# A plain first block by token halves in the inner SwiGLUs, TensorE's order at the norms written out, and turned tiles split straight from PSUM

## The chip, the cores and the metric

The kernel runs on one core of a Trainium2 chip. Its time is the device time of one execution in microseconds, and a version is judged by the median of its runs. The profiled execution is one further run, with its own time and span.

The engines in the profile are PE (TensorE, matrix products and transposes; PEld is its loading of weights), DVE (VectorE), ACT (ScalarE), POOL (GpSimd) and SP (SyncE). SP issues most loads; POOL issues loads and the DMAs that add into a tile.

## The reference

The input x is 512 tokens of 1024 features, in fp32. There are two layers, and a final norm.

```python
def rms_norm(x, gain):
    inv = lax.rsqrt(jnp.mean(xf * xf, axis=-1, keepdims=True) + NORM_EPS)
    return (xf * inv).astype(x.dtype) * gain

def swiglu(h, w_gate, w_up, w_down):
    return (jax.nn.silu(h @ w_gate) * (h @ w_up)) @ w_down

for l in range(DEPTH):
    x = x + 0.5 * swiglu(rms_norm(x, ffn1_norm[l]), ffn1_wg[l], ffn1_wu[l], ffn1_wd[l])
    h = rms_norm(x, mix_norm[l])
    z = h @ w_in[l]
    ...
    x = x + jnp.concatenate([attn_out, conv_out], axis=-1) @ w_out[l]
    x = x + 0.5 * swiglu(rms_norm(x, ffn2_norm[l]), ffn2_wg[l], ffn2_wu[l], ffn2_wd[l])
return rms_norm(x, final_norm)
```

The hidden width of a SwiGLU is 2816. The mixing between the two SwiGLUs of a layer is a sliding-window attention beside a short convolution.

## The kernel before

**Numbers.** Every fp32 operand of a matrix product is kept as two parts, hi (a rounded copy, written by ACT) and lo (the rest, a subtraction on DVE); `split` (L203 to L205) makes them. A product is three matmuls: hi by hi, hi by lo, lo by hi. Weights come by DMA into tiles `raw` (8 buffers, `need_raw`, L190) and are split into `wh` and `wl` (3 buffers each, `need_split`, L213, with the split at L204 and L205). A unit of weights is 512 KB. `split_far` (L207 to L211) makes lo in another way: ACT writes hi and the negated source, and a DMA issued by POOL adds the source to it.

**Stages.** The 2816 hidden columns are 11 blocks of 256. A SwiGLU is a list of stages (L32 to L40). `p` is a plain block (gate and up, four groups of 128 columns over all eight chunks of 128 features). `w` is a pair of blocks done with seven half-size products instead of eight (`winograd2`, L926), in the order of CHAINS: the accumulators x, w, x, y, x, y, x take the operands b11, b21, t2, t3, t1, t4, b22. The operands are quarters of the normed, turned activations (chunks 0 to 3 or 4 to 7, first or second half of the 512 tokens), and t1 to t4 are sums of quarters; `Seven.make` (L567) forms and splits one, once. `u` is one block done in the same way with matmuls of 256 columns (`winograd`, L867, matmuls at L896). `s` is the down-projection of four blocks, again with seven products (`share`, L790, through `stream`, L775, matmuls at L781). `d` is the plain down-projection of the blocks listed (`down`, L300, matmuls at L309). Three SwiGLUs use INNER (FFN2 of layer 0, FFN1 and FFN2 of layer 1; the last with another ending, LAST, whose list is the same); FFN1 of layer 0 uses FIRST. Where a `w` block's result is needed with the features on the partitions, `turn` (L979) transposes it on TensorE, and `flush` empties the list of turns that wait, some per step.

**The norm.** `Norm` is called after each piece of the residual stream x is final (L504): ACT squares it with a row sum (L506). When the four pieces of one half of the tokens are there, `stage` (L522) forms the root (L529 to L532), and for each of the four pieces `turn` (L541) scales it (xn, L546, DVE), transposes it in four blocks into a PSUM tile (L551) and copies the tile out: to the full tile hf for a SwiGLU (L557, on ACT or DVE), or split into hh and hl for the mixing. For a SwiGLU, `stage` then makes b11 and b21 from the first half, and t2 after the second.

**PSUM.** The pools are "mm" (4 banks), "sc" (2) and "aux" (2). The tiles of the eight turns take their banks from a list of tags (L1385, L1386): aux, aux, sc, sc for the first half, then mm, mm, sc, sc ahead of a SwiGLU and sc, sc, aux, aux ahead of the mixing.

**The mixing** (`mix`, L1177) runs its first three groups of w_in by token halves: all three over the first 256 tokens, then all three over the second (L1186 to L1199, matmuls of 256 columns). Its output projection is a `share` whose operands t1, t4 and b22 are split far (L1181). The pieces of x that it ends go to the next norm: that is where FFN2's norm begins, during the last steps of `share`.

**Order.** The tile framework's scheduler decides in which order each engine gets its instructions, here for PE too; only the last stage of all has its order on ACT and DVE written by hand (L1160).

Of the kernel before, what the change touches and what calls it, by code (L numbers as in the profile page):

```python
# [15 lines left out]
P = 128  # L16
# [20 lines left out]
    ("w", 0), ("w", 2), ("w", 4), ("w", 6), ("w", 8), ("u", 10), ("s", 0), ("s", 4),  # L37
    ("d", (8, 9, 10)),
)
LAST = INNER[:-1] + (("d", (8, 9, 10)),)  # L40
# [32 lines left out]
def trunk_kernel(  # L73
# [226 lines left out]
    def down(acts, blocks):  # L300
# [167 lines left out]
    class Norm:  # L468
# [19 lines left out]
        def rooms(self):  # L488
            if self.mixing:
                self.parts = [  # L490
# [7 lines left out]
            else:  # L498
# [3 lines left out]
                self.make, self.forms = self.seven.make, self.seven.forms  # L502

# [18 lines left out]
        def stage(self, half):  # L522

            i = self.i
            if half == 0:
                self.rooms()
            v, r, y = (small(f"{n}_{i}_{half}", 2) for n in "vry")
# [5 lines left out]
            for o in range(2):  # L533
                for t in (at, at + 1):
                    self.turn(t, o, y[:, t - at : t - at + 1])
                if half == 0 and not self.mixing:
                    self.make(("b11", "b21")[o])
            if half and not self.mixing:
                self.make("t2")

        def turn(self, t, o, by):  # L541
# [3 lines left out]
            xn = g2(f"xn_{name}")  # L545
            nc.vector.scalar_tensor_tensor(  # L546
                xn, xt(t, o), by, self.gain[o], op0=ALU.mult, op1=ALU.mult
            )
# [3 lines left out]
            if self.mixing:  # L552
                hi, lo = (p[:, :, tok] for p in self.parts[o])
                nc.scalar.copy(hi, tp)
                nc.vector.tensor_sub(lo, tp, f32(hi))
            else:
                (nc.vector.tensor_copy if o else nc.scalar.copy)(self.full[o][:, :, tok], tp)  # L557
# [217 lines left out]
    def stream(accs, wh, wl, xh, xl, h, start):  # L775

        for u in range(2):
            tok = slice(u * P, (u + 1) * P)
            for k in range(2):
                for i, (x_, w) in enumerate(((xh, wh), (xl, wh), (xh, wl))):  # L780
# [7 lines left out]
                    )  # L788

    def share(ops, by, between=None, soon=None, after=None):  # L790
# [34 lines left out]
    def ffn(norm, stages, whole, after=None, late=None):  # L825
# [4 lines left out]
        def plain(b):  # L830
# [34 lines left out]
            acts[b] = (hi, lo)  # L865

# [59 lines left out]
        def winograd2(b, between=None):  # L926
# [12 lines left out]
            for step, (acc, operand, start) in enumerate(CHAINS):  # L939
# [32 lines left out]
                if not first and step < 4:  # L972
# [452 lines left out]
```

## Time and profile before

| what | value |
|---|---|
| median of 3 runs | 1727.09 us (1723.63 to 1728.24) |
| the profiled execution | 1727.49 us |
| its span in the profile | 1725.7 us |
| mean granted TensorE clock | 0.992 |
| instructions | 21836 |

A line of the timeline gives start, duration, engine, line of the program, operation, the tile written and the tiles read, and in brackets the idle time of the engine just before it with what ended it. Names lose their buffer numbers: `ft_m` is any of the sums t1 to t4 of the mixing's projection, `fb_m` a plain quarter of it, `y_s` an accumulator of a down-projection share, `w`, `x` and `y` those of a pair of blocks, `acc` that of a plain group. "x2" after a line counts neighbouring instructions of one form, which the view merges even where other matmuls lie between. A duration of a matmul includes its way through the array, so the time that one costs in a row is the distance between two starts. A row of the windows view gives, for a stretch, the busy time and the count of instructions of each engine, the granted clock, the DMA share and the rate.

### The profile page before, as it was taken

The page shows a single profiled execution, that of the slowest core. Times are in us where ns is not written, and L with a number is a line of the kernel's source. Part 1 is how long each engine was busy: PE and PEld are TensorE (multiplying, and loading weights), DVE is VectorE, ACT ScalarE, POOL GpSimd, SP SyncE. Part 2 cuts the span into 40 slices and gives each one's busy share as a digit, 9 for nine tenths or more (in the row PEclk, how much of TensorE's full clock was granted, in tenths as well). Part 3 has the DMA queues.
Part 4 walks back from the last instruction along what each step waited for, and adds up shares of the span by engine and source line. Part 5 has one row for each costly group of instructions (what it writes and reads, how often), then busy time and mean ns, then how long its engine had stood idle before and what let it go on. Part 6 is the DMA issues. An engine that isn't in the chain of part 4 may idle for free.

```text
span 1725.7 us, 21836 instructions
## 1 busy us (share of the span) xinstructions
PE 1685.2 (98%) x8150; PEld 1405.2 (81%) x8150; DVE 1345.7 (78%) x1762; ACT 959.5 (56%) x1369; POOL 191.8 (11%) x172
## 2 busy tenths in 40 slices
PE   9999999999988999999999999999999799999998
PEld 7888898898867888887778888878888678888877
DVE  7986689868779777799597776995578797776994
ACT  6545555556565555564455555644565655556553
POOL 0011111000210111011101111110002101111101
PEclk9999999999999999999999999999999989999999
DMA  8467788622694767678547776783127947767781
GB/s 244 103 180 194 183 205 210 166 66 62 153 225 123 207 172 189 179 191 222 147 122 196 186 180 184 191 219 112 39 74 166 212 133 191 188 171 190 189 207 49
DMA packets 188206, 285.62 MB, mean 166 GB/s; under 512 B 9124, under 2 KB 72132, under 8 KB 188100
## 3 DMA queue, kind: packets, MB, share of 16 engines
q1 hardware_dynamic: 146340, 204.91, 37.6%
q0 software_dynamic: 41056, 78.65, 26.9%
q8 instruction: 64, 1.05, 0.2%
q10 hardware_dynamic: 704, 0.66, 0.1%
q14 instruction: 42, 0.34, 0.1%
HBM read 268.46 MB, written 2.10 MB: 157 GB/s over the span
## 4 chain that ended last, share of the span: by engine, by line
PE 59%; DVE 6%; issue 2%; ACT 1%; DMA 1%; POOL 0%; ACTq 0%; POOLq 0%; DVEq 0%
PE x L781 18%; PE y L781 9%; PE x_s L781 6%; PE w L781 4%; PE y_s L781 4%; PE down L309 3%; PE x L896 2%; PE acc L291 2%; PE acc L292 2%; PE acc L294 2%; PE at L982 2%; DVE wl L205 1%; PE y L896 1%; DVE raw L231 1%; PE acc L1192 1%
## 5 line engine op out<-in xcount | busy, mean ns | idle before, releaser
L204 ACT CAST wh<-raw 128x1024 fp32r<-128x1024 f32 (+1 forms) x503 | 524.4, 1045 | 557.4 <-PE x L781 137.6
L205 DVE TENSOR_TENSOR wl<-raw,wh 128x1024 fp32r<-128x1024 f32 (+1 forms) x503 | 606.6, 1213 | 269.1 <-ACT wh L204 267.5
L781 PE MATMUL x<-wh,ft 128*128 128x512 f32 x608 | 189.6, 392 | 1.0 <-DVE ft L205 1.0
L781 PE MATMUL x<-wh,fb 128*128 128x512 f32 x608 | 188.5, 390 | 0.0
L781 PE MATMUL y<-wh,ft 128*128 128x512 f32 x608 | 188.5, 391 | 0.0
L781 PEld LDWEIGHTS x<-wh,ft 128*128 128x128 f32 x608 | 113.1, 188 | 25.1 <-DVE ft L205 2.2
L781 PEld LDWEIGHTS x<-wh,fb 128*128 128x128 f32 x608 | 114.3, 188 | 23.4
L781 PEld LDWEIGHTS y<-wh,ft 128*128 128x128 f32 x608 | 113.1, 188 | 22.7
L781 PE MATMUL x<-wl,fb 128*128 128x512 f32 x304 | 118.6, 390 | 0.0
L781 PE MATMUL x<-wl,ft 128*128 128x512 f32 x304 | 118.4, 390 | 0.0
L781 PE MATMUL y<-wl,ft 128*128 128x512 f32 x304 | 118.3, 389 | 0.0
L199 POOL DMA_DIRECT2D raw<-in_ffn_wu_dram x42 | 51.1, 1217 | 585.6 <-DMA raw<-in_ffn_wu_dram 405.2
L781 PE MATMUL w<-wh,fb 128*128 128x512 f32 x304 | 98.6, 409 | 5.3 <-ACT wh L204 5.3
L291 PE MATMUL acc<-hh,wh 128*128 128x512 f32 x240 | 94.6, 394 | 0.0
L294 PE MATMUL acc<-hh,wl 128*128 128x512 f32 x240 | 93.9, 391 | 0.0
L292 PE MATMUL acc<-hl,wh 128*128 128x512 f32 x240 | 93.6, 390 | 0.0
L309 PE MATMUL down<-wh,a 128*128 128x512 f32 x288 | 90.0, 392 | 0.0
L781 PE MATMUL y_s<-wh,ft_s 128*128 128x512 f32 x256 | 80.5, 392 | 5.4 <-ACT wh L204 5.4
L781 PE MATMUL x_s<-wh,ft_s 128*128 128x512 f32 x256 | 78.1, 393 | 1.2 <-ACT wh L204 1.0
L199 POOL DMA_DIRECT2D raw<-in_ffn_wg_dram x42 | 50.9, 1219 | 244.6 <-DVE wl L205 92.3
L781 PE MATMUL x_s<-wh,fb_s 128*128 128x512 f32 x240 | 74.0, 389 | 0.0
L781 PEld LDWEIGHTS w<-wh,fb 128*128 128x128 f32 x304 | 57.4, 195 | 19.6 <-ACT wh L204 8.2
(313 smaller groups left out, 3451.3 us busy)
## 6 DMA issues: line engine op xcount, KB each, us to landing
raw<-in_ffn_wu_dram SPq DMA_DIRECT2D x129, 512.0 KB, 3.7
raw<-in_ffn_wd_dram SPq DMA_DIRECT2D x104, 512.0 KB, 5.4
raw<-in_ffn_wg_dram SPq DMA_DIRECT2D x86, 512.0 KB, 5.0
raw<-in_ffn_wu_dram POOLq DMA_DIRECT2D x42, 512.0 KB, 7.7
raw<-in_ffn_wg_dram POOLq DMA_DIRECT2D x42, 512.0 KB, 6.3
raw<-in_w_in_dram SPq DMA_DIRECT2D x36, 512.0 KB, 3.8
raw<-in_ffn_wd_dram POOLq DMA_DIRECT2D x32, 512.0 KB, 7.8
raw<-raw POOLq DMA_DIRECT2D x20, 512.0 KB, 6.4
```

The costliest lines, as they stand in the source:

```text
L199: nc.gpsimd.dma_start(out=r, in_=rows_of(*more), accum_op=ALU.add)
L204: nc.scalar.copy(hi, raw)
L205: eng.tensor_sub(lo, raw, f32(hi))
L231: nc.vector.tensor_add(a11, a11, s1)
L291: nc.tensor.matmul(acc, hi[:, k, :], rhs[k][0], start=k == first, stop=False)
L292: nc.tensor.matmul(acc, hi[:, k, :], rhs[k][1], start=False, stop=False)
L294: nc.tensor.matmul(acc, lo[:, k, :], rhs[k][0], start=False, stop=k == last)
L309: nc.tensor.matmul(acc, a[:, k, tok], w[:, k, :], start=i + k + n == 0, stop=i == last and k == 1 and n == 2,)
L781: nc.tensor.matmul(accs[u], x_[:, 2 * h + k, tok], w[:, k, :], start=start and h + k + i == 0, stop=h + k == 2 and i == 2, skip_group_chec ...
L896: nc.tensor.matmul(out, w[:, k, cols], x_[:, k, :], start=start and k + i == 0, stop=k == KC // 2 - 1 and i == 2, skip_group_check=not start,)
L982: nc.tensor.transpose(tp[:, t * P : (t + 1) * P], ups[t][:, c * P : (c + 1) * P], ident)
L1192: nc.tensor.matmul(opened[j][:, tok], w[:, k, :], x_, start=t + k + i == 0, stop=k == KC - 1 and i == 2, skip_group_check=True,)
```

## The change

The list INNER begins with a plain block (0), five pairs follow (1, 3, 5, 7, 9), the shares cover blocks 1 to 4 and 5 to 8, and the plain down-projection takes 0, 9 and 10. The `u` stage is gone from these three SwiGLUs.

A new function `halves` runs three groups by token halves, as the mixing did, and serves both: after the second group of the first half, and in the middle of the third, it calls `norm.pull`. The plain block (`plain_halves`) is these three groups (two gates, one up), and then the second up group.

`stage` now makes the xn of a half at once and leaves the turns to `pull`, which does one pair of turns. The pulls stand in the program's order at fixed places: in the last step of the share that ends the stream (after each of its four runs of six matmuls), or after the pieces of the last down-projection, and in `halves`. From step 4 of that share, or from the second half of the down-projection, to the end of the plain block (or of the three groups of the mixing), TensorE's order is the program's (`by_hand` to `by_itself`).

A turned tile ahead of a SwiGLU is split from its PSUM bank: ACT copies hi, DVE subtracts lo, both into the operand b11, b21, b12 or b22, and ACT copies the tile in full into hf as well, for the sums. t2, t3 and t1 are made as the plain block's groups end, t4 after it. In the mixing's projection t4 is no longer split far.

In the second of the shares, the turns of the last pair (9) are flushed one per step in steps 2 to 5, into an "aux" bank.

```diff
@@ -34,10 +34,10 @@
     ("s", 2), ("d", (10,)), ("s", 6),
 )
 INNER = (
-    ("w", 0), ("w", 2), ("w", 4), ("w", 6), ("w", 8), ("u", 10), ("s", 0), ("s", 4),
-    ("d", (8, 9, 10)),
+    ("p", 0), ("w", 1), ("w", 3), ("w", 5), ("w", 7), ("w", 9), ("s", 1), ("s", 5),
+    ("d", (0, 9, 10)),
 )
-LAST = INNER[:-1] + (("d", (8, 9, 10)),)
+LAST = INNER[:-1] + (("d", (0, 9, 10)),)
 FORMS = ("a11", "a12", "s2", "s3", "s1", "a22", "s4")
 EARLY = ("a11", "a12", "s3", "s2", "a22", "s1", "s4")
 SCORES_AT = (5, 6, 7, 8, 9, 10, 12, 13)
@@ -297,7 +297,38 @@
                 nc.tensor.matmul(acc, lo[:, k, :], rhs[k][0], start=False, stop=k == last)
         return acc
 
-    def down(acts, blocks):
+    def by_hand():
+        state["region"] = tc.manual_schedule(engines={pe})
+        state["region"].__enter__()
+
+    def by_itself():
+        state["region"].__exit__(None, None, None)
+
+    def halves(norm, n, done):
+
+        first = state["group"]
+        held = [take_split(SPLIT_AHEAD - j)[1:] for j in range(n)]
+        accs = [psum("mm", [P, S], f"acc_{first + j}") for j in range(n)]
+        for t in range(2):
+            for j, (hi, lo) in enumerate(held):
+                for k in range(KC):
+                    xh, xl = norm.half(k, t)
+                    for i, (w, x_) in enumerate(((hi, xh), (hi, xl), (lo, xh))):
+                        nc.tensor.matmul(
+                            accs[j][:, t * H : (t + 1) * H],
+                            w[:, k, :],
+                            x_,
+                            start=t + k + i == 0,
+                            stop=k == KC - 1 and i == 2,
+                            skip_group_check=True,
+                        )
+                    if t == 0 and (j, k) in ((1, KC - 1), (2, KC // 2 - 1)):
+                        norm.pull()
+                if t:
+                    need_split(first + j + 3)
+                    done(j, accs[j])
+
+    def down(acts, blocks, norm=None):
 
         last = len(blocks) - 1
 
@@ -316,6 +347,8 @@
 
         for o in range(2):
             accs = [psum("mm", [P, S], f"down_{state['group']}_{t}") for t in range(NT)]
+            if o and norm:
+                by_hand()
             if o and last:
                 held = [take_split(SPLIT_AHEAD - i)[1:] for i in range(last + 1)]
                 ahead = state["group"]
@@ -328,6 +361,8 @@
                         products(accs[t], t, i, *w)
                         if i == last:
                             yield t, o, accs[t]
+                            if norm:
+                                norm.pull()
                     need_split(ahead + i)
                 continue
             for i in range(last + 1):
@@ -487,6 +522,7 @@
 
         def rooms(self):
             if self.mixing:
+                self.half = lambda k, t: [z[:, t * H : (t + 1) * H] for z in self.h[k]]
                 self.parts = [
                     [
                         xpool.tile([P, KC // 2, S], F32R, tag="xf", bufs=8, name=f"h{n}_{self.i}_{o}")
@@ -500,6 +536,9 @@
                 self.full = full
                 self.seven = Seven(full, room_g8, f"{self.i}")
                 self.make, self.forms = self.seven.make, self.seven.forms
+                self.half = lambda k, t: [
+                    z[:, k % 4, :] for z in self.forms[f"b{k // 4 + 1}{t + 1}"]
+                ]
 
         def __call__(self, t, o):
 
@@ -524,6 +563,7 @@
             i = self.i
             if half == 0:
                 self.rooms()
+                self.waiting = []
             v, r, y = (small(f"{n}_{i}_{half}", 2) for n in "vry")
             at = 2 * half
             nc.vector.tensor_add(v, self.ss[:, at : at + 2], self.ss[:, NT + at : NT + at + 2])
@@ -531,30 +571,46 @@
             nc.vector.tensor_scalar(v, v, 1.0 / D, EPS, op0=ALU.mult, op1=ALU.add)
             newton(y, r, v)
             for o in range(2):
+                xns = []
                 for t in (at, at + 1):
-                    self.turn(t, o, y[:, t - at : t - at + 1])
-                if half == 0 and not self.mixing:
-                    self.make(("b11", "b21")[o])
-            if half and not self.mixing:
-                self.make("t2")
-
-        def turn(self, t, o, by):
+                    xns.append(g2(f"xn_{i}_{t}_{o}"))
+                    nc.vector.scalar_tensor_tensor(
+                        xns[-1],
+                        xt(t, o),
+                        y[:, t - at : t - at + 1],
+                        self.gain[o],
+                        op0=ALU.mult,
+                        op1=ALU.mult,
+                    )
+                self.waiting.append((half, o, xns))
+
+        def pull(self):
+
+            if not self.waiting:
+                return
+            half, o, xns = self.waiting.pop(0)
+            for t, xn in enumerate(xns):
+                self.turn(2 * half + t, o, xn)
+
+        def turn(self, t, o, xn):
 
             name = f"{self.i}_{t}_{o}"
             tok = slice(t * P, (t + 1) * P)
-            xn = g2(f"xn_{name}")
-            nc.vector.scalar_tensor_tensor(
-                xn, xt(t, o), by, self.gain[o], op0=ALU.mult, op1=ALU.mult
-            )
             tp = psum(self.tags.pop(0), [P, KC // 2, P], f"xt_{name}")
             for j in range(KC // 2):
                 nc.tensor.transpose(tp[:, j, :], xn[:, j * P : (j + 1) * P], ident)
             if self.mixing:
                 hi, lo = (p[:, :, tok] for p in self.parts[o])
-                nc.scalar.copy(hi, tp)
-                nc.vector.tensor_sub(lo, tp, f32(hi))
             else:
-                (nc.vector.tensor_copy if o else nc.scalar.copy)(self.full[o][:, :, tok], tp)
+                what = f"b{o + 1}{t // 2 + 1}"
+                if what not in self.forms:
+                    self.forms[what] = both(f"f{what}_{self.i}")
+                at = t % 2 * P
+                hi, lo = (p[:, :, at : at + P] for p in self.forms[what])
+            nc.scalar.copy(hi, tp)
+            nc.vector.tensor_sub(lo, tp, f32(hi))
+            if not self.mixing:
+                nc.scalar.copy(self.full[o][:, :, tok], tp)
 
     class Seven:
 
@@ -772,7 +828,7 @@
                 bias[:, h, :], df, -(2.0 ** -(h + 1)), m0, op0=ALU.mult, op1=ALU.add
             )
 
-    def stream(accs, wh, wl, xh, xl, h, start):
+    def stream(accs, wh, wl, xh, xl, h, start, norm=None):
 
         for u in range(2):
             tok = slice(u * P, (u + 1) * P)
@@ -786,6 +842,8 @@
                         stop=h + k == 2 and i == 2,
                         skip_group_check=not start,
                     )
+            if norm:
+                norm.pull()
 
     def share(ops, by, between=None, soon=None, after=None):
 
@@ -794,13 +852,15 @@
         chains, shares = (CHAINS_EARLY, SHARES_EARLY) if after else (CHAINS, SHARES)
         for step, (acc, operand, start) in enumerate(chains):
             ops.make(operand)
+            if after and step == 4:
+                by_hand()
             xh, xl = ops.forms[operand]
             if start:
                 tag = {"x": "mm", "y": "sc", "w": "aux", "z": "mm"}[acc]
                 accs[acc] = [psum(tag, [P, S], f"{acc}_{ops.name}_{m}") for m in range(2)]
             for h in range(2):
                 _, wh, wl = take_split()
-                stream(accs[acc], wh, wl, xh, xl, h, start)
+                stream(accs[acc], wh, wl, xh, xl, h, start, after if step == 6 else None)
                 if soon:
                     ops.make(*soon.get((step, h), ()))
                 if h == 0:
@@ -863,6 +923,43 @@
                 norm.make("t2")
                 up(1, accs[3])
             acts[b] = (hi, lo)
+
+        def plain_halves(b):
+
+            gates = [g2(f"gate_{whole}_{b}_{j}") for j in range(2)]
+
+            def up(j, acc):
+                nc.vector.tensor_mul(gates[j], acc, gates[j])
+                if not j:
+                    acts[b] = both(f"a_{whole}_{b}", shape=(P, 2, 2, S))
+                hi, lo = acts[b]
+                split(hi[:, j, :], lo[:, j, :], gates[j])
+
+            def done(j, acc):
+                if j < 2:
+                    nc.scalar.activation(gates[j], acc, AF.Silu)
+                else:
+                    up(0, acc)
+                norm.make(("t2", "t3", "t1")[j])
+
+            halves(norm, 3, done)
+            _, hi, lo = take_split()
+            acc = psum("mm", [P, S], f"up_{whole}_{b}")
...
+            up(1, acc)
+            by_itself()
+            norm.make("t4")
 
...
@@ -969,8 +1066,6 @@
                             nc.scalar.activation(gates[2 + u], out, AF.Silu)
                             nc.vector.tensor_mul(ups[2 + u], ups[2 + u], gates[2 + u])
                 turns(step)
-                if not first and step < 4:
-                    norm.make(("t3", "t1", "t4", "b22")[step])
                 if between:
                     between(step)
             if b in blocks:
@@ -1031,9 +1126,14 @@
                     ops, 0.5, ahead(then, {3: ("b11",), 4: ("b21",), 5: sums[:1], 6: sums[1:]})
                 )
             elif what == "s":
-                share(then, 0.5, after=after if final else None)
+                share(
+                    then,
+                    0.5,
+                    None if first else lambda step: 2 <= step < 6 and flush(1, "aux"),
+                    after=after if final else None,
+                )
             if what == "p":
-                plain(b)
+                (plain if first else plain_halves)(b)
                 if b == 0 and late:
                     turn_rows(1)
             if what != "d":
@@ -1043,8 +1143,8 @@
                     [(acts[k][0][:, j, :], acts[k][1][:, j, :]) for k in b for j in range(2)]
                 )
                 return
-            for n, (t, o, acc) in enumerate(down(acts, b)):
-                if b == (0,):
+            for n, (t, o, acc) in enumerate(down(acts, b, after if final else None)):
+                if b == (0,) and first:
                     norm.make(*{0: ("t3",), 4: ("t1",)}.get(n, ()))
                 nc.vector.scalar_tensor_tensor(
                     xt(t, o), acc, 0.5, xt(t, o), op0=ALU.mult, op1=ALU.add
@@ -1178,27 +1278,12 @@
         q = [None] * NH
 
         mixed = [g8(f"m_{l}_{j}", F32, (P, KC // 2, S)) for j in range(2)]
-        ops = Seven(mixed, room_g8, f"m_{l}", far=("t1", "t4", "b22"))
-
-        first = state["group"]
-        held = [take_split(SPLIT_AHEAD - j) for j in range(3)]
-        kacc, vacc, qacc = opened = [psum("mm", [P, S], f"acc_{n}") for n, _, _ in held]
...
+        ops = Seven(mixed, room_g8, f"m_{l}", far=("t1", "b22"))
+
+        opened = []
+        halves(norm, 3, lambda j, acc: opened.append(acc))
+        by_itself()
+        kacc, vacc, qacc = opened
 
         kh, kl = both(f"k_{l}", shape=(P, 2, NKV, S))
         kh, kl = ([t[:, g, :] for g in range(NKV)] for t in (kh, kl))
```

More of the change, by code (lines that the diff above doesn't have):

```diff
@@ L865, in plain @@
             acts[b] = (hi, lo)
+        def plain_halves(b):
[15 more added lines that the diff above has]
+            acc = psum("mm", [P, S], f"up_{whole}_{b}")
+            for t in range(2):
+                for k in range(KC):
+                    xh, xl = norm.half(k, t)
+                    for i, (w, x_) in enumerate(((hi, xh), (hi, xl), (lo, xh))):
+                        nc.tensor.matmul(
+                            acc[:, t * H : (t + 1) * H],
+                            w[:, k, :],
+                            x_,
+                            start=t + k + i == 0,
+                            stop=k == KC - 1 and i == 2,
+                            skip_group_check=True,
+                        )
+            up(1, acc)
+            by_itself()
+            norm.make("t4")
         def winograd(b, between):
```

17 lines of the change are left out of this document (1 added, 16 removed).

## The prediction

> **What bounds the kernel now.** The page first:
>
> ```profile
> span 1725.7 us, 21836 instructions
> PE 1685.2 (98%) x8150; PEld 1405.2 (81%) x8150; DVE 1345.7 (78%) x1762; ACT 959.5 (56%) x1369; POOL 191.8 (11%) x172
> PE   9999999999988999999999999999999799999998
> PEclk9999999999999999999999999999999989999999
> PE 59%; DVE 6%; issue 2%; ACT 1%; DMA 1%; POOL 0%; ACTq 0%; POOLq 0%; DVEq 0%
> ```
>
> TensorE (PE) sets the time: it is busy for 98% and carries 59% of the chain that ended last. Its row has dents at slices 11 and 12 and near slice 32, and the clock row has one at the latter. So two questions decide: how much matmul time the change adds, and what happens in the dents. For the first I need pitches, start to start, from the timeline and from the list of one line (duration: min/median/max):
>
> ```profile
> 720.29 0.39 PE L781 MATMUL x<-wl,fb 128*128 128x512 f32 x1
> 720.97 0.39 PE L781 MATMUL x<-wl,fb 128*128 128x512 f32 x1
> 729.90 0.28 PE L896 MATMUL w<-fb,wl 128*128 128x256 f32 x1
> 730.26 0.28 PE L896 MATMUL w<-fb,wl 128*128 128x256 f32 x1
> 353.00 0.60 PE L551 MATMUL xt<-ident,xn 128*128 128x128 f32 x4
> L551 PE MATMUL xt<-ident,xn x160: 270/273/421, 337.7 to 1390.8; 128*128 128x128 f32 x160
> ```
>
> Between the first two rows, as between the next two, lie three starts (one hi·lo triple): 0.68/3 = 0.227 us for 512 columns, 0.36/3 = 0.120 us for 256. Four transposes last 0.60 us, one 0.27: (0.60-0.27)/3 = 0.11 us each.
>
> For the second, three stretches of the windows view (PE busy with count, then PEld, DVE, ACT, POOL, clock, DMA share, GB/s), around the norms ahead of l0's FFN2, l1's FFN1 and l1's FFN2:
>
> ```profile
> 475.00:550.00 75.00, 64.07 (x272) 50.41 (x272) 64.31 (x80) 46.52 (x66) 7.85 (x7) 0.93 0.69 164
> 850.00:900.00 50.00, 46.17 (x205) 36.12 (x205) 45.74 (x57) 30.35 (x41) 3.61 (x3) 0.97 0.33 88
> 1325.00:1400.00 75.00, 64.59 (x269) 50.85 (x269) 61.50 (x76) 42.70 (x58) 12.48 (x11) 0.91 0.72 162
> ```
>
> Each holds the norm's 32 transposes (8 turned tiles of four), the rest are 512 wide. At full pitch the first needs 240 x 0.227 + 32 x 0.11 = 57.9 us of its 75: **17.1 us lost**. Likewise 173 x 0.227 + 3.5 = 42.7 of 50, **7.3 lost**, and 237 x 0.227 + 3.5 = 57.2 of 75, **17.8 lost**. TensorE's waits say on what:
>
> ```profile
> PE y_m L781 <- DMA ft_m<-sums_m: 9.5, 2, 4.9
> PE w L781 <- DVE wl L205: 7.2, 4, 2.7
> PE y_s L781 <- ACT wh L204: 5.4, 6, 0.9
> PE w L781 <- ACT wh L204: 5.3, 6, 0.9
> PE x_m L781 <- DVE wl L205: 1.7, 2, 0.9
> PE x_s L781 <- ACT wh L204: 1.0, 4, 0.3
> ```
>
> and the timeline and windows of l0's FFN2 norm show them in order, with half clock behind them:
>
> ```profile
> 491.46 0.39 PE L781 MATMUL y_m<-wh,ft_m 128*128 128x512 f32 x1
> 496.47 1.22 PE L781 MATMUL y_m<-wh,ft_m 128*128 128x512 f32 x2 [4.62 <-DMA ft_m<-sums_m]
> 518.52 1.19 PE L781 MATMUL w<-wh,fb 128*128 128x512 f32 x4 [0.93 <-ACT wh L204]
> 522.46 0.79 PE L781 MATMUL w<-wl,fb 128*128 128x512 f32 x1 [2.74 <-DVE wl L205]
> 526.95 0.50 PE L781 MATMUL w<-wh,fb 128*128 128x512 f32 x1 [0.87 <-ACT wh L204]
> ```
> ```profile
> 496.50:504.00 7.50, 7.50 (x22) 5.96 (x23) 1.77 (x2) 1.05 (x1) 2.42 (x2) 0.64 0.82 220
> 518.00:530.00 12.00, 7.80 (x27) 5.43 (x28) 11.23 (x17) 3.62 (x8) 0.00 (x0) 0.86 0.27 45
> 870.00:876.00 6.00, 6.00 (x28) 4.97 (x29) 5.22 (x8) 1.18 (x2) 0.00 (x0) 0.72 0.00 0
> ```
>
> First the mixing's t4 operand is late by DMA, then the pair w0 starves for split weights: a 12-matmul half takes 2.7 us, and meanwhile ACT and DVE, which owe it a pair (casts and subtractions below), also turn and split the norm. The clock 0.64 over 7.5 us costs 2.7 us, 0.86 over 12 costs 1.7. A pause of 4.62 us costs 5.01-0.23-4.62 = 0.16 more for the restart.
>
> **The change part by part.**
>
> *Plain block for one-block pair (+8.6).* u10 is seven steps of 24 matmuls, 168; the plain block runs 4 groups x 8 chunks x 3 products x 2 token halves = 192, all 256 wide. +24 in each of three SwiGLUs: 72 x 0.120 = **+8.6 us**, at 98% busy not hidden. Fewer forms and combinations for DVE and ACT are worth nothing by themselves.
>
> *t4 near instead of far (inside the -10.7 and -11.4 below).* 4.62 us and their half clock go in both mixings; in exchange DVE gets one subtraction (1.22 below) where it waits anyway. t1 stays far, and is safe: its DMA was issued 2.5 us ahead of t4's, behind which t4's had to queue, and is wanted one step (24 x 0.227 = 5.4 us) after t4.
>
> ```profile
> 484.41 1.29 POOL L211 DMA_DIRECT2D ft_m<-m  x1 [8.15 <-ACT ft_m L209]
> 486.92 0.88 POOL L211 DMA_DIRECT2D ft_m<-sums_m  x1 [1.22 <-ACT ft_m L209]
> ```
>
> *Norms.* Durations in the old norm, from the timelines:
>
> ```profile
> 505.27 0.62 ACT L506 ACTIVATE sq<-x 128x512 bf16<-128x512 f32 x1
> 505.80 0.19 ACT L506 ACTIVATION_READ_ACCUMULATOR sq<-x 128x1 f32 x1
> 507.17 1.03 ACT L204 CAST wh<-raw 128x1024 fp32r<-128x1024 f32 x1
> 509.46 1.26 ACT L557 COPY hf<-xt 128x512 f32<-128x512 f32 x2 [1.25 <-PE xt L551]
> 506.78 0.16 DVE L529 TENSOR_TENSOR v<-ss 128x2 f32<-128x2 f32 x1
> 507.96 2.74 DVE L546 SCALAR_TENSOR_TENSOR xn<-x,y,gain 128x512 f32<-128x512 f32 x4
> 510.61 1.22 DVE L205 TENSOR_TENSOR wl<-raw,wh 128x1024 fp32r<-128x1024 f32 x1
> 512.98 1.28 DVE L557 COPY hf<-xt 128x512 f32<-128x512 f32 x2
> ```
>
> A plain group with its weight pair lasts 48 x 0.120 = 5.8 us against 2.7 for a pair's half, so casts and subtractions (about 1.05 and 1.2 each) fit: I cost w0's waits at zero. What is late next, by the built order:
> - *The second half's xn.* The first turn of it stands behind two groups of the first half, 5.8 us after the last step. ACT meanwhile has a weight cast (1.03), two full copies (1.26) and two squares (2 x 0.81) in front of the root; v to xn takes 507.96-506.78 = 1.2, the first xn 0.7, about eight hand-offs 0.15 each 1.2: 7.0. **1.2-1.4 late.**
> - *A shared bank.* The third group's accumulator lies in the PSUM bank of the first late tile (both "mm"), so TensorE waits for that tile's three readings, hi copy, lo subtraction, full copy. The subtraction is queued behind the other three xn (2.0 us), then 0.64, the copy 0.63, hand-offs 0.2; less two turns and waits that TensorE spends itself (1.2): **2.2**. Queued behind it on TensorE: third group, last turns, second half.
> - *Clock*: two such pauses within 4 us: between 0 and 2.7, I take **1.5** (nearest the 1.7 of 518:530). *Left from before*: x_m's wait, 0.88 + 0.16 = **1.05**. Small ones: **0.3**.
>
> Sum 1.35 + 2.15 + 1.5 + 1.05 + 0.3 = 6.4: **-10.7** at l0's FFN2 norm and **-11.4** at l1's. At l1's FFN1 norm the down block's end (d 0,9,10) precedes; there ACT must send b21's first hi copy behind a square, two full copies, a cast and a root (0.81+1.26+1.03+0.3), about 3.0 late at the fifth chunk of the first group; then the bank 1.6, clock 1.5, 0.3: 6.4 for 7.3, **-0.9**. In l1's mixing norm, of the same form without full copies, the same queue costs **+1.3**; l0's stays.
>
> [...]
>
> The nearest rows for the new stage as a whole are mixing's norms, which already run their first groups by token halves:
>
> ```profile
> 335.00:372.00 37.00, 36.81 (x246) 33.24 (x245) 26.93 (x44) 21.92 (x37) 0.00 (x0) 1.00 0.32 94
> 1212.00:1250.00 38.00, 38.00 (x228) 33.72 (x228) 19.27 (x40) 20.91 (x36) 0.00 (x0) 1.00 0.10 28
> ```
>
> There TensorE loses nearly nothing: the lower bound per norm is about 1-2 us. The upper is what stands today, 17, 7 and 17. I stay near the lower, since three readings, not two, hang on each tile.
>
> *Down-projection shares (-8.1).* y_s's and x_s's waits: 5.4 + 1.0 and ten restarts x 0.16. They exist because y_s's first product stands ahead of x_s's lo products, and its cast waits for a weight buffer that is still in use. In the built order of after, each pair's products finish before the next begins; w9's turned tiles flushed in s5 add nothing to TensorE. I take it as gone; bound: still there, 0.
>
> **Sum**: +8.6 - 10.7 - 11.4 - 0.9 + 1.3 - 8.1 = -21.2. The profiled execution took 1727.49 us (span 1725.7 and 1.8 around it); 0.4 above the median of the runs shown. 1727.49 - 21.2 = 1706.3, **1706** against the median.
>
> **Rivals.**
> - *Norms nearly free.* The bank's wait is covered and the clock stays: 2 us a norm instead of 6.4, three norms, -13: **1693**. For it: the mixing rows. Against: a hard-written order cannot fill the waits.
> - *Shares keep their waits* under another name (cast against buffer): +8, **1714**. For it: ACT casts are what those rows name; against: the order.
> - *Queues replace queues.* At the FFN norms only t4's DMA and its clock go (4.62 + 0.16 + 2.7 = 7.5 twice), ACT's and DVE's backlog costs as today: norms -15 instead of -23: **1714**; with the shares' waits, 1722.
> - *Slower: half clock through the norms.* The written order makes TensorE pause where the scheduler would have put other matmuls. If the pauses throttle it for the whole plain block, 192 x 0.120 = 23 us more in each of three norms less the 1.5 counted, +64: 1771; if only for the first-half groups of 72 matmuls, 8.6-1.5 = 7.1 each, +21: **1728**. It decides from 21.2/3 = 7 us more per norm. For it: 0.72 in 870:876, after waits of only about 1 us each. Against: clock 1.00 in both mixing rows.
> - *Nothing gained where it matters* (waits move one stage on): 1727.
>
> [...]
>
> **How the numbers follow.** Forecast 50%; norms nearly free 16%; shares 11%; queues 11%; slower 9%; nothing gained 3%. The forecast's own range is 1701 to 1711 (clock 0 to 2.7 in three norms, the late xn half or double). The range runs from 1693, which halves the free case, to 1718, above both 1714s: left out are slower, nothing and half the free case, 20%. What this measurement can tell from no change is 0.3%, 5.2 us. Faster: 50+16+11+11 less a tail of 1 = 0.87; same 0.04 (nothing gained, some of that tail); slower 0.09.
>
> **What would show it.** No y_m wait on a DMA and no w waits at the FFN norms; in their place waits of the transposes for xn, and of acc for the full copy L613 or its bank, about 2 us; clock 0.8-0.95 there. No y_s waits on casts. 72 more matmuls of 256 columns. The three stretches lose about 6 us each. Wrong would be: a long wait at the first transposes, a clock below 0.7 through the plain block, or losses over 12 us in a stretch.

## The result, and the profile after

| | before | after |
|---|---|---|
| median | 1726.48 us (1723.63 to 1728.24, 4 runs) | 1699.44 us (1699.30 to 1701.48, 4 runs) |
| ratio | | 0.9848, 95% interval 0.9831 to 0.9865 |
| span of the profiled execution | 1725.7 us | 1699.7 us |

The change makes the kernel 27.0 us faster; 1706 was forecast, with a range of 1693 to 1718. The median lies inside that range, but below the forecast's own narrower one of 1701 to 1711. The page of after:

```profile
span 1699.7 us, 21898 instructions
PE 1679.4 (99%) x8222; PEld 1412.8 (83%) x8222; DVE 1323.5 (78%) x1734; ACT 953.2 (56%) x1361; POOL 182.2 (11%) x164
PE   9999999999999999999999999999999999999998
PEclk9999999999999999999999999999999999999999
PE 94%; DVE 4%; ACT 1%; issue 0%; DMA 0%; SPq 0%; DVEq 0%; ACTq 0%
```

The dents are gone from PE's row and the clock's; TensorE carries 94% of the chain instead of 59%, with 72 matmuls more (8222 for 8150). Its waits:

```profile
PE acc L317 <- ACT hf L613: 5.4, 3, 1.9
PE acc L317 <- ACT fb L610: 1.6, 1, 1.6
PE x_m L837 <- DVE wl L205: 1.5, 2, 0.8
PE xt L700 <- DMA x<-in_x_dram: 1.3, 1, 1.3
...
PE acc L317 <- DVE hl L611: 0.7, 1, 0.7
PE xt L601 <- DVE xn L577: 0.7, 3, 0.3
...
PE acc L317 <- ACT hh L610: 0.4, 1, 0.4
```

No y_m wait on a DMA, no w wait, no y_s wait is left. The fourth line is the kernel's start, where a load came late in this execution (its time, 1701.48, is the slowest of the four; the start costs about 2 us: the first L291 matmul begins at 29.45 us, in before at 27.11). The first line is the shared bank, once per non-mixing norm. The timeline at l0's FFN2 norm, then at l1's, each followed by its row of the windows view:

```profile
517.78 1.32 PE L601 MATMUL xt<-ident,xn 128*128 128x128 f32 x8 [0.19 <-DVE xn L577]
520.98 0.80 PE L317 MATMUL acc<-fb,wh 128*128 128x256 f32 x2 [1.89 <-ACT hf L613]
...
518.00:530.00 12.00, 10.11 (x72) 9.63 (x71) 7.07 (x10) 5.44 (x9) 1.20 (x1) 0.86 0.40 88
```
```profile
1362.28 1.32 PE L601 MATMUL xt<-ident,xn 128*128 128x128 f32 x8 [0.20 <-DVE xn L577]
1365.48 0.50 PE L317 MATMUL acc<-fb,wh 128*128 128x256 f32 x2 [1.88 <-ACT hf L613]
...
1356.00:1370.00 14.00, 11.91 (x96) 11.19 (x95) 10.22 (x19) 8.47 (x17) 2.30 (x2) 1.00 0.77 192
```

The same two waits stand in both; only the first is followed by half clock (0.50 granted in 521:524; 0.14 x 12 = 1.7 us), while l1's has 1.00 in 1356:1370. What the 1.89 us at l0's norm consist of, from DVE's and ACT's timeline:

```profile
516.97 2.74 DVE L577 SCALAR_TENSOR_TENSOR xn<-x,y,gain 128x512 f32<-128x512 f32 x4
519.62 1.28 DVE L611 TENSOR_TENSOR fb<-xt,fb 128x512 fp32r<-128x512 f32 x2
520.34 1.18 ACT L613 COPY hf<-xt 128x512 f32<-128x512 f32 x2 [0.63 <-DVE fb L611]
```

The subtraction stands behind all four xn, and the full copy starts (520.34) when the first subtraction is over (519.62 + 0.69 = 520.31); ACT's idle 0.63 us ended with it. So this tile's readings followed one another here, as the prediction's sum has them; what makes them do so was not tested. At l1's FFN1 norm, TensorE's waits and ACT's queue ahead of the late hi copies of b21:

```profile
854.11 0.39 PE L317 MATMUL acc<-fb,wh 128*128 128x256 f32 x1 [1.55 <-ACT fb L610]
854.91 0.39 PE L317 MATMUL acc<-fb,wh 128*128 128x256 f32 x1 [0.41 <-DVE fb L611]
863.32 0.50 PE L317 MATMUL acc<-fb,wh 128*128 128x256 f32 x2 [1.58 <-ACT hf L613]
...
846.00:858.00 12.00, 10.04 (x59) 8.95 (x58) 11.06 (x20) 7.70 (x15) 0.82 (x1) 0.88 0.50 144
```
```profile
849.67 0.63 ACT L545 ACTIVATE sq<-x 128x512 bf16<-128x512 f32 x1
850.30 0.56 ACT L613 COPY hf<-xt 128x512 f32<-128x512 f32 x1
850.76 1.05 ACT L204 CAST wh<-raw 128x1024 fp32r<-128x1024 f32 x1
851.71 0.58 ACT L613 COPY hf<-xt 128x512 f32<-128x512 f32 x1
852.19 0.64 ACT L545 ACTIVATE sq<-x 128x512 bf16<-128x512 f32 x1
852.81 0.58 ACT L610 CAST fb<-xt 128x512 fp32r<-128x512 f32 x1
853.28 0.31 ACT L570 ACTIVATE r<-v,eps 128x2 f32<-128x2 f32 x1
853.48 0.59 ACT L610 CAST fb<-xt 128x512 fp32r<-128x512 f32 x1
```

### The profile page after: what moved, and what is told of

Same layout as the page of the kernel before. It is cut to its first block, busy times and chain, and to the rows that moved or that the text cites. A ratio compares the mean times of both kernels' runs of the same rounds, so it can differ in the third digit from the quotient of the medians.

```text
span 1699.7 us, 21898 instructions
## 1 busy us (share of the span) xinstructions
PE 1679.4 (99%) x8222; PEld 1412.8 (83%) x8222; DVE 1323.5 (78%) x1734; ACT 953.2 (56%) x1361; POOL 182.2 (11%) x164
## 4 chain that ended last, share of the span: by engine, by line
PE 94%; DVE 4%; ACT 1%; issue 0%; DMA 0%; SPq 0%; DVEq 0%; ACTq 0%
PE x L837 24%; PE y L837 12%; PE x_s L837 10%; PE w L837 6%; PE down L340 6%; PE y_s L837 5%; PE acc L317 4%; PE acc L291 4%; PE acc L292 4%; PE acc L294 4%; PE w_s L837 3%; PE at L1077 2%; PE x_m L837 2%; DVE wl L205 1%; PE up L952 1%; PE acc L735 1%
## 5 line engine op out<-in xcount | busy, mean ns | idle before, releaser
L204 ACT CAST wh<-raw 128x1024 fp32r<-128x1024 f32 (+1 forms) x494 | 516.3, 1046 | 563.4 <-PE x L837 126.4
L205 DVE TENSOR_TENSOR wl<-raw,wh 128x1024 fp32r<-128x1024 f32 (+1 forms) x494 | 597.6, 1212 | 243.0 <-ACT wh L204 241.2
L199 POOL DMA_DIRECT2D raw<-in_ffn_wu_dram x39 | 47.2, 1210 | 539.6 <-DMA raw<-in_ffn_wu_dram 407.5
L837 PE MATMUL w<-wh,fb 128*128 128x512 f32 x304 | 95.2, 394 | 0.0
L291 PE MATMUL acc<-hh,wh 128*128 128x512 f32 x240 | 94.6, 394 | 0.0
L199 POOL DMA_DIRECT2D raw<-in_ffn_wg_dram x39 | 47.0, 1213 | 265.6 <-DMA raw<-in_ffn_wu_dram 97.5
L231 DVE TENSOR_TENSOR raw<-raw,raw 128x1024 f32<-128x1024 f32 x58 | 70.5, 1219 | 0.5
```

The source lines that it names most:

```text
L199: nc.gpsimd.dma_start(out=r, in_=rows_of(*more), accum_op=ALU.add)
L204: nc.scalar.copy(hi, raw)
L205: eng.tensor_sub(lo, raw, f32(hi))
L231: nc.vector.tensor_add(a11, a11, s1)
L291: nc.tensor.matmul(acc, hi[:, k, :], rhs[k][0], start=k == first, stop=False)
L837: nc.tensor.matmul(accs[u], x_[:, 2 * h + k, tok], w[:, k, :], start=start and h + k + i == 0, stop=h + k == 2 and i == 2, skip_group_chec ...
```

## The experiments

The ratio of each is to the kernel before on the same chip, whose median was 1725.69, 1725.98 and 1724.80 us in the three sets. The change itself was measured in another set (before: 1726.48), so a difference to the change, taken between medians, can be off: by the ratios these differences come out up to 1 us otherwise.

**t4 alone** (in the kernel before), and **t4 undone** (in the changed kernel):

```diff
-        ops = Seven(mixed, room_g8, f"m_{l}", far=("t1", "t4", "b22"))
+        ops = Seven(mixed, room_g8, f"m_{l}", far=("t1", "b22"))
```


> The kernel before with one edit: t4 of the mixing's projection is split on ACT and DVE, not by a DMA. My theory: at both FFN2 norms the y_m wait on a DMA goes (4.6 and 4.9 us) with its restart and the half clock behind it (about 2.4 each); w0's waits stay, since DVE stood idle for 7 us there. About -14: 1712 us, and the stretch from 475 to 550 loses 10 us instead of 17. Rival: the added subtraction makes DVE late for the next weights, and y_m waits for DVE instead: -6 to -8, 1719 us. Second rival: the time won is lost again at w0, which then starves earlier: 1726 us.

Measured 1711.16 us, ratio 0.9914 (0.9899 to 0.9929): **-14.5**, as the theory has it. The stretch:

```profile
475.00:550.00 75.00, 69.52 (x305) 55.40 (x303) 72.17 (x87) 48.83 (x68) 9.40 (x8) 0.95 0.72 177
```

273 x 0.227 + 3.5 = 65.5 of 75: 9.5 us lost instead of 17.1; w0's waits remain. In the old kernel this one word is worth more than half of what the whole change brings. The reverse edit in the changed kernel:

> The changed kernel with t4 of the mixing's projection split far again. My theory: y_m waits 4.6 to 5 us for the DMA at both FFN2 norms, with half clock behind it (2.4 us each): +14, 1713 us. Rival: the written order and the earlier issue change the DMA's time, and less than half of the wait returns: 1705 us or less.

1710.94 us, 0.9913 (0.9898 to 0.9927): +11.5, between the theory and the rival. So t4 is worth 14.5 us in the old kernel and 11.5 in the changed one. TensorE's waits show the DMA again, somewhat shorter than before (9.5):

```profile
PE y_m L837 <- DMA ft_m<-sums_m: 6.8, 2, 3.6
```

**The shares' order alone** (in the kernel before: `share` inside a region in which PE's order is the program's, final shares excepted):

```diff
+        region = None if after else tc.manual_schedule(engines={pe})
+        if region:
+            region.__enter__()
...
+        if region:
+            region.__exit__(None, None, None)
```


> The kernel before with one edit: TensorE's order in the down-projection shares of the SwiGLUs (all but those that end a stream) is that of the program. My theory: y_s's and x_s's waits in the three shares come from the scheduler's order, in which y_s's first product stands ahead of x_s's lo products: 10 waits with about 6.4 us and their restarts go, -8 to -10: 1717 us. Rival: ACT and DVE are late there whatever the order, and the waits come back under x_s on the split weights: 1726 us.

1729.74 us, 1.0024 (1.0014 to 1.0033), slower by 4. The y_s waits are gone, and this stands in their place:

```profile
PE x_s L781 <- DVE wl L205: 8.1, 6, 1.5
```

The theory fell: the scheduler's order was not the cause, it softened a DVE that was late. A new theory took its place.

**The one-block pair ahead of the last pair** (in the kernel before; also `winograd` called where no share follows, and pair 9's turns flushed in the second share):

```diff
-    ("w", 0), ("w", 2), ("w", 4), ("w", 6), ("w", 8), ("u", 10), ("s", 0), ("s", 4),
+    ("w", 0), ("w", 2), ("w", 4), ("w", 6), ("u", 8), ("w", 9), ("s", 0), ("s", 4),
```


> The kernel before with the one-block pair moved ahead of the last pair (INNER: pairs 0, 2, 4, 6, one block 8, pair 9, shares 0 and 4, plain 8, 9, 10) and pair 9's turned tiles flushed in the second share, as the change does. Norms, plain block and t4 are as before. The theory that scheduling alone makes the shares' waits has fallen; the new one: DVE enters the share late because the share's first operands are formed beside the one-block pair, which asks for weights every 2.9 us at 256 columns a matmul; beside a full pair they have twice the time. So y_s's and x_s's waits go in all three shares, -8 to -10: 1717 us. Rival: it was the plain block's or the other blocks' lighter load on DVE, and the waits stay: 1726 us.

1714.71 us, 0.9941 (0.9926 to 0.9956): **-10.1**, and no share wait is left. The windows of the stage ahead of the share and of the share's first 18 us, before and here (third pair of numbers: DVE):

```profile
725.30:747.20 21.90, 21.90 (x186) 21.90 (x185) 20.34 (x26) 15.37 (x24) 4.16 (x4) 1.00 0.76 193
747.20:765.00 17.80, 16.79 (x74) 13.26 (x73) 17.71 (x20) 10.37 (x12) 2.41 (x3) 1.00 0.70 123
```
```profile
705.60:743.70 38.10, 38.10 (x170) 31.57 (x169) 36.62 (x38) 25.46 (x31) 2.42 (x3) 1.00 0.71 190
743.70:761.70 18.00, 18.00 (x81) 14.89 (x80) 17.85 (x21) 11.78 (x12) 4.17 (x4) 1.00 0.95 218
```

DVE is full in the share both times, and no less busy ahead of it (20.34 of 21.90, 36.62 of 38.10): its load is not what differs. Its work is. In before, u10's own end lies at the share's start, two splits of a among it:

```profile
749.51 0.68 DVE L205 TENSOR_TENSOR a<-up,a 128x512 fp32r<-128x512 f32 x1
...
751.85 0.69 DVE L205 TENSOR_TENSOR a<-up,a 128x512 fp32r<-128x512 f32 x1
```

The last pair's a is split later, in the second share, and DVE has the weight sums (L231) and wl done earlier. So the shares' gain needs no plain block: it comes with the place of the `u` stage and the later turns of the pair, which this edit moves together. Whether u10's splits, the pair's splits or the operands formed beside u10 made DVE late was not separated.

**No written order** (in the changed kernel, `by_hand` and `by_itself` empty):

```diff
-        state["region"] = tc.manual_schedule(engines={pe})
-        state["region"].__enter__()
+        pass
...
-        state["region"].__exit__(None, None, None)
+        pass
```


> The changed kernel without the written order: by_hand and by_itself do nothing, the scheduler places TensorE's instructions at the norms. My theory: most of the gain at the norms comes from the plain block by token halves, which asks for weights half as often, and from t4; the scheduler's order costs or gains little: 1697 to 1704 us. Rival: the written order carries the gain, since the scheduler puts the transposes late or early as it did in the kernel before: 1710 us or more.

1689.95 us, 0.9792 (0.9777 to 0.9806): **9.5 us faster than the change**, more than either theory allowed. The scheduler changes two things. The late turns come ahead of the third group (at l0's FFN2 norm all but the last four transposes, which follow two matmuls later). And at l1's FFN1 norm, while b21 is late, it runs the second group's b11 products: its first wait there comes after 23 matmuls (845.62 to 848.85, 0.23 us), in after it comes after 12 (850.89 to 854.11, 1.55 us). The late turns at l0's FFN2 norm, the wait for the full copy that is left there, and the clock:

```profile
514.99 2.04 PE L600 MATMUL xt<-ident,xn 128*128 128x128 f32 x12 [0.20 <-DVE xn L576]
518.20 0.51 PE L316 MATMUL acc<-fb,wh 128*128 128x256 f32 x2 [0.27 <-ACT hf L612]
...
509.00:521.00 12.00, 11.43 (x90) 10.35 (x89) 10.75 (x20) 7.98 (x17) 2.41 (x2) 1.00 0.69 186
```

0.27 us for 1.89, and full clock.

**Both late pulls after the second group**, order still by hand:

```diff
-                    if t == 0 and (j, k) in ((1, KC - 1), (2, KC // 2 - 1)):
+                    if t == 0 and (j, k) == (1, KC - 1):
+                        norm.pull()
                         norm.pull()
```


> The changed kernel, order still written by hand, with both pulls of the second half after the second group, so that the third group follows all four turns, as the scheduler puts it when left alone. If it is the place of the pulls that costs, the bank's wait and its half clock go at the FFN2 norms and the FFN1 norm keeps its wait for b21 (2.4 us, with half clock 1.5): -5, 1694 us. If a fixed order costs as such, whatever its places: 1699 us.

1696.02 us, 0.9832 (0.9816 to 0.9849); 3.4 less than after, 2.8 by the ratios. The place of the pulls costs about a third of the 9.5; the bank's wait shrinks from 5.4 to 3.2, and b21's stays. The granted clock is 1.00 at l0's FFN2 norm (484:530) and at l1's FFN1 norm (838:866), and x_m's two waits are 1.2 us longer than in after (2.7 for 1.5), which takes back a part:

```profile
PE acc L317 <- ACT hf L614: 3.2, 3, 1.2
PE acc L317 <- ACT fb L611: 1.6, 1, 1.6
```

**Own banks** and **late full copies** (in the changed kernel), each alone and both:

```diff
-        late = ("sc", "sc", "aux", "aux") if mixing else ("mm", "mm", "sc", "sc")
+        late = ("sc", "sc", "aux", "aux") if mixing else ("sc", "sc", "aux", "aux")
```
```diff
-                nc.scalar.copy(self.full[o][:, :, tok], tp)
+                self.later.append((self.full[o][:, :, tok], tp))
...
+            if o and not self.mixing:
+                for full, tp in self.later:
+                    nc.scalar.copy(full, tp)
+                self.later = []
```


> The changed kernel with the tags of the second half's turned tiles changed from mm, mm, sc, sc to sc, sc, aux, aux, as ahead of the mixing: the third accumulator shares no bank with them. My theory: TensorE's waits for the full copy (2.05, 2.05 and 1.74 us in the profile of after, with restart) go, and the half clock behind the first (1.5 us): -6 to -7, 1693 us. Rival: the wait moves on to the second half's operands, which DVE subtracts behind the same four xn, and little is won: 1698 us.

1691.61 us, 0.9798 (0.9784 to 0.9813): **-7.8**; the wait for hf is gone from the list, and nothing takes its place:

```profile
PE acc L317 <- ACT fb L610: 1.6, 1, 1.6
...
PE xt L601 <- DVE xn L577: 0.9, 3, 0.3
```

> The changed kernel with the full copies of a half put behind both pairs of turns in the program. My theory: ahead of FFN1 of layer 1, b21's hi copies no longer stand behind two full copies of ACT, 1.2 us less of the 2.4 us wait and some of its half clock; the bank's wait stays or grows by 0.6: -1 to -2, 1698 us. Rival: ACT's square, weight cast and root decide there, not the copies: 1699 to 1700 us.

1697.63 us, 0.9835 (0.9821 to 0.9850), 1.8 less than after: as expected in size, but not by the expected way. b21's two waits at the FFN1 norm fall only from 1.96 to 1.59 us (0.89 and 0.70), not by 1.2: ACT's weight cast (847.06) and square (848.00) still stand in front of the hi copies, as the rival has it. Most of the rest is the clock: at that norm it is 1.00 (836:860) where after has 0.93, 1.7 us. The last section shows that this can fall either way.

> Both edits, own banks and late full copies. If the two waits are independent, as my theory has it: -7 to -9, 1691 us. Rival: the late copies hold the banks that the second half's tiles now take, and a wait at the transposes takes back a part: 1695 us or more.

1691.45 us, 0.9801 (0.9783 to 0.9819): the size that the theory gave, yet no better than own banks alone. b21's waits are as short as with late full copies (0.88 and 0.71), but the clock at that norm is again 0.93 (836:860). So the 1.8 us of the late copies were mostly the clock, and the rival's +4 did not come.

**Whole operands split from hf**, not from the bank (in the changed kernel):

```diff
-                what = f"b{o + 1}{t // 2 + 1}"
...
-                hi, lo = (p[:, :, at : at + P] for p in self.forms[what])
+                (nc.vector.tensor_copy if o else nc.scalar.copy)(self.full[o][:, :, tok], tp)
+                if t % 2:
+                    self.make(f"b{o + 1}{t // 2 + 1}")
+                return
             nc.scalar.copy(hi, tp)
             nc.vector.tensor_sub(lo, tp, f32(hi))
-            if not self.mixing:
-                nc.scalar.copy(self.full[o][:, :, tok], tp)
...
-                src = {"b11": b11, "b21": b21, "b22": b22, "t1": b12}.get(what)
+                src = {"b11": b11, "b12": b12, "b21": b21, "b22": b22, "t1": b12}.get(what)
```


> The changed kernel with the turned tiles copied to hf once (ACT for the first four chunks, DVE for the last four, as in the kernel before) and b11, b21, b12, b22 split from hf as whole operands. My theory: the operands come 1.5 to 2 us later (a cast of 1.05 and a subtraction of 1.2 over 1024 columns behind the copy, where 0.6 and 0.65 do now), at the first group and again where the second half begins, while the shared bank is free after one reading: +2 to +4 at each of three norms, 1706 to 1711 us. Rival: with one reading instead of three the bank's wait of 1.7 to 2.1 us goes and pays for it: 1699 us.

1702.76 us, 0.9867 (0.9852 to 0.9882): +3.3, between the two. The bank's wait falls from 5.4 to 0.7, and the operands come later:

```profile
PE acc L317 <- DVE fb L205: 7.1, 7, 1.3
PE acc L317 <- ACT fb L204: 1.6, 4, 0.5
...
PE acc L317 <- ACT hf L605: 0.7, 3, 0.2
```

**Whole tokens** (no written order, the plain block's first three groups each over all tokens):

```diff
-        for t in range(2):
-            for j, (hi, lo) in enumerate(held):
+        whole = not norm.mixing
+        if whole:
+            norm.pull()
+            norm.pull()
+        for t, j in [(t, j) for j in range(n) for t in range(2)] if whole else [
+            (t, j) for t in range(2) for j in range(n)
+        ]:
+            for hi, lo in held[j : j + 1]:
```


> The changed kernel without the written order (1690 us), and the three first groups of the plain block each over all 512 tokens in turn instead of three over the first half, then three over the second; the mixing keeps its halves. If the token halves carry the norms' gain, TensorE now waits for the second half's norm, about 7 us of squares, root, xn and turns and some 3 of splitting less one first-half group of 2.9, with half clock behind: +7 to +11 at each of three norms, 1711 to 1723 us. If the gain came from weights being asked for half as often: within 3 us of 1690.

1708.47 us, 0.9905 (0.9891 to 0.9920): **+18.5** on 1689.95, some 6 a norm: a little below the first theory's range (1711 to 1723), and far from the second. TensorE waits for the second half, once per norm, and the transposes behind that wait run at half the rate at l0's FFN2 norm (16 in 3.68 us, 0.23 each, for 0.11 in before):

```profile
PE xt L606 <- DVE xn L582: 16.7, 3, 6.0
514.37 3.68 PE L606 MATMUL xt<-ident,xn 128*128 128x128 f32 x16 [5.95 <-DVE xn L582]
```

The halves carry most of the norms' gain. The price is an upper one: the edit also puts both late pulls ahead of the first group, and no matmul of that group runs in the wait, though its first half (24 x 0.120 = 2.9 us) was ready. A plain block in front seems worth little without them: t4 and the `u` stage alone, and the plain block's matmuls, give an estimate of 1724.8 - 14.5 - 10.1 + 8.6 = 1709, about what this kernel takes.

**No written order and own banks**, the two gains together:

> The changed kernel without the written order and with own banks for the second half's turned tiles. The scheduler's order already fills most of the bank's wait (0.5 us left): 1689 us, within 1 us of the kernel without the written order. If the late tiles now wait for the first half's readings in their banks: 1691 us or more.

1686.01 us (1685.83 to 1686.24), 0.9774 (0.9759 to 0.9789): the fastest here, 13.4 us below the change and 38.8 below before. It beats the expectation by 3: with own banks the scheduler also moves third-group products between the late turns, and no wait for xn or hf is left in the list of waits. From l0's FFN2 norm:

```profile
515.03 0.63 PE L600 MATMUL xt<-ident,xn 128*128 128x128 f32 x4
515.41 0.36 PE L316 MATMUL acc<-fb,wh 128*128 128x256 f32 x1
```

Beside the start, x_m's two waits (1.6 us) are the longest.

## Why the prediction was right, and where its sizes were off

| step | predicted | measured |
|---|---|---|
| plain block | +8.6 | +8.6 (72 matmuls more) |
| l0's FFN2 norm | 17.1 to 6.4: -10.7 | to 5.2: -11.9 |
| l1's FFN2 norm | 17.8 to 6.4: -11.4 | to 3.5: -14.3 |
| l1's FFN1 norm | 7.3 to 6.4: -0.9 | to 5.7: -1.6 |
| l1's mixing norm | +1.3 | +0.7 (1.3 lost in 1165:1210, 0.6 before in 1190:1240) |
| shares | -8.1 | -10.1 (b_u_early, by the moved `u` stage) |

The measured column adds up to -28.6; the medians differ by 27, the spans by 26, and after's profiled execution lost 2.3 us at its start, so 28.3 without the start. Counting the matmuls of the traces, as the prediction did, gives nearly the same: 4.9 us lost in 475:550 (l0's FFN2 norm), 3.6 in 1325:1400 (l1's), 5.4 in 840:880 (FFN1's), and 3.0 to 3.2 less in the rest of each of the three SwiGLUs. Measured losses in the table are the waits shown, 0.16 per restart (the figure of before's 4.62 us pause), and the clock: at l0's FFN2 norm 0.77 (x_m) + 0.19 + 1.89 + 3 x 0.16 + 0.2 (a second, shorter xn wait) + 1.7 = 5.2; at l1's without the clock 3.5; at FFN1's 1.55 + 0.41 + 1.58 + 0.5 + 1.4 + 0.3 (0.12 x 12, and 0.04 x 8 behind it).

Right in mechanism and size: t4 (b_t4_near), the shared bank (1.89 + 0.16 for 2.15; a_own_banks), w0's waits gone. Right in mechanism, smaller in size: b21's hi copies behind ACT's queue (the instructions named, though the root comes only between the two hi copies; 1.55 + 0.41 and two restarts, 2.3, for 3.0). Two of the sums do not add up as written: the bank's terms give 2.27, not 2.15, and ACT's queue 3.4, not 3.0. Neither changes the forecast much. That the copy must stand behind the subtraction, its 0.63 us added to the bank's wait, no run shows; it was the author's estimate, and in after the copy does start 0.03 us after the subtraction's end.

Off in size: *the late xn*, 0.2 to 0.5 for 1.2 to 1.4. The step put the weight cast and both full copies in front of the squares; in the trace they are done before the last piece of x is there, and count for nothing. No run shows the 0.15 us for each of eight hand-offs; in after, ACT's root starts 0.04 us after v's end, DVE goes on 0.03 after the root's, and the transposes start 0.06 after the first xn's (517.72 to 517.78). *The clock*, 1.5 in each norm: 1.7 in two, nothing in the third. Of the 7.4 us by which the measured column lies below the sum of -21.2, the late xn makes 2.0 (1.35 against 0.35, twice), the clock 1.1 and the shares 2.0; the rest is small terms.

Wrong in its reason: *the shares*. The step held the order of TensorE's products for the cause. b_share_hand replaced that order by the program's and the kernel became 4 us slower; the waits came from DVE's lateness behind the `u` stage, and b_u_early took them away and left the order to the scheduler. That the size (-8.1 for -10.1) came out nearly right is luck: the change happened to move that stage, too.

Seen, but not priced: *the written order*. The forecast kept the bank's wait because "a hard-written order cannot fill the waits", and the rival "slower" feared pauses where the scheduler would have put other matmuls. Both name the cost, but neither compares it with the scheduler's own order, and that is 9.5 us: a_no_hand (1690) is about what the rival "norms nearly free" (1693) described, and it is the change's own written order that keeps it from that.

## What to carry to other kernels

A change of several parts should be run part by part: here t4 near and the `u` stage moved bring 14.5 and 10.1 us, each measured alone in the old kernel with a small edit, the token halves pay for the plain block and more, and the written order takes 9.5 back. Before an engine's order is written out by hand, run the scheduler's; where it must be written, put work whose inputs are ready ahead of work that shares a bank with a tile in turn. An operand should not be split by a DMA where TensorE wants it sooner than the DMA lands: t4 was wanted 4.9 us after the issue, and the matmul that waited for it started 9.5 us after it (486.92 to 496.47); t1's DMA, issued 2.5 us ahead of t4's, landed in 7.7.

## What the runs showed of the hardware

Whether a pause of about 2 us throttles TensorE is not settled by its length. In after, 1.89 us at l0's FFN2 norm is followed by half clock (0.50 in 521:524), and 1.88 at l1's is not (1.00 in 1356:1370). With late full copies, the same pauses stand at the same places, and it is the other way round:

```profile
518.66 0.50 PE L317 MATMUL acc<-fb,wh 128*128 128x256 f32 x2 [1.89 <-ACT hf L597]
1359.95 0.51 PE L317 MATMUL acc<-fb,wh 128*128 128x256 f32 x2 [1.89 <-ACT hf L597]
...
515.00:527.00 12.00, 9.90 (x81) 9.23 (x80) 8.45 (x12) 6.13 (x10) 1.20 (x1) 1.00 0.59 122
1358.00:1370.00 12.00, 10.11 (x72) 10.06 (x72) 7.44 (x10) 5.69 (x10) 1.20 (x1) 0.86 0.34 65
```

What decides it, no run here shows. The idle time just ahead of the pause does not: in after it is 0.19 us where half clock follows, and 0.20 where it does not. So differences of some 2 us between such kernels can be the clock's alone (0.14 x 12 = 1.7 us here), and removing a pause can win more than its length (own banks: 7.8 us won, where the waits were 5.4).
